# A transformer block on one core: the beginning reordered, tokens laid out by grid tiles, the first weights in pieces of 128 rows

## The chip, the core and the metric

The kernel runs on one core of a Trainium2 chip. A core has five engines with queues of their own: TensorE (PE; its weight loads are shown as PEld), VectorE (DVE), ScalarE (ACT), GpSimd (POOL) and SyncE (SP), which here only issues transfers. Sixteen DMA engines move data between HBM and the on-chip memory (SBUF). TensorE writes its products into PSUM, eight banks of 128 x 512 f32. The metric is the device time of one execution in microseconds (us).

## The reference

One layer of a block with modulation, for 1024 tokens (a grid of 16 rows by 64 columns) of width 1024 and 256 context tokens. What matters for the beginning:

```python
mod_x = (silu(c) @ w_mod + b_mod)            # six rows of 1024: sh1, sc1, gt1, sh2, sc2, gt2
mod_c = silu(c_ctx) @ w_mod + b_mod
h_x = rmsnorm(x, g_pre_mix) * (1 + sc1) + sh1
h_c = rmsnorm(ctx, g_pre_mix) * (1 + csc1) + csh1
u, q, k, v = split(h_x @ w_in)               # u: 512 columns, then three times 512
...
mix = concat(pool_mixer(u), neighbourhood_attention(q, k, v, k_ctx, v_ctx)) @ w_out
x = x + gt1 * rmsnorm(mix, g_post_mix)
x = x + gt2 * rmsnorm(relu(modulate(x) @ w_mlp_in)**2 @ w_mlp_out, g_post_mlp)
```

## The kernel before

All large products are made in three parts, since each operand is split into a high part (fp32r) and a low part: high x high, high x low, low x high (`three`, L197; in the beginning `some_sums`, L444). `high_part` (L144) is a copy on ScalarE, `low_part` (L150) a subtraction on VectorE.

The change lies in the beginning (L271 to L501), where the instructions of TensorE, ScalarE, VectorE, SP and GpSimd keep the order in which they are written (`in_order`, L104, entered at L284). It runs so:

- **Loads on SP** (L303 to L308): eight token tiles `x0` to `x7` of 128 tokens x 1024, 512 KB each; then, for each quarter q of the modulation, four pages of `w_mod` (`mod_load`, L297: 512 rows of K by 256 columns, for shift and scale) and the two K chunks 2q, 2q + 1 of `w_in`'s first 512 columns as one load (`raw_u`); then the context.
- **Normalisation**: a square with a running sum on ScalarE (`mean_square`, L130), then `rsqrt_of` (L133): an addition on VectorE and a power on GpSimd; then the tile is multiplied on VectorE (`normalised`, L333). `squares` of tile n + 1, with its inverse root, is written ahead of `normalised` of tile n (L368).
- **Transposes** on TensorE (`turned`, L343) of each 128 x 128 block, four tokens tiles side by side in a PSUM bank for each K chunk k and half h. `spare` (L339) puts transposes of the identity in between, whose results nobody reads.
- **Copies** out of PSUM (`by_bands`, L348) into `xT[k]`, 128 x 1024, on ScalarE or VectorE. The attention later works on tiles of 16 rows by 8 columns of the grid, so these copies also reorder the tokens from rows to such tiles. A token half `b` (512 columns of `xT`) needs both token halves of the input.
- **Modulation** of quarter q (256 of 1024 channels, K chunks 2q and 2q + 1 of the next product): `mod_sums` (L396) is 16 matmuls of `sT` (silu of c and c_ctx, 32 columns) against 256 columns; `mod_kept` copies the row; `shift_scale` (L415) turns it into columns by two small matmuls with `pck` (four PE instructions) and makes `a1` (scale) and `s1` (shift) by six small VectorE instructions.
- **`latent(b, k)`** (L431, through `modulated`, L202): ScalarE makes the high part, VectorE the f32 value and the low part; for b = 1 ScalarE also makes the f32 value and VectorE only the low part.
- **Products of u**: `some_sums(b, js, k)`, three matmuls of 128 x 512 for each of the output groups js: four for half 0, two for half 1, summed over k = 0 to 7 in the banks `pu`. The loop at L483 takes two values of k at a time, with the next quarter's modulation in between.

PSUM holds six banks that pass from tile to tile (`ps1`) and two for tiles named in `bank` (L273; `ps_t`, "lasting"). A tile that asks for a bank gets it when the one that had it has been read for the last time.

Later parts that the change touches: L548 to L550 rebuild `xT[0]` and `xT[1]` of half 0 by an addition (their f32 value was not kept in place), and the last stores (L1947) write rows back through the view `og` of the output.

Of the kernel before, what the change touches and what calls it, by code (L numbers as in the profile page):

```python
# [69 lines left out]

def _pick_table():
# [9 lines left out]
def hybrid_block(ctx, tc, x, ctx_in, w_mod, b_mod, gp1, gp2, w_in, pool_w, rpb, w_out, w1, w2, vectors,  # L81
# [37 lines left out]
    tiles = lambda a: a.rearrange("(r m c) d -> m r c d", r=QR, m=NM)  # L119
# [151 lines left out]
    with tc.tile_pool(name="ps1", bufs=6, space=PSUM) as ps1, tc.tile_pool(name="tmp1", bufs=3) as tmp:  # L271

        def bank(name):  # L273
            if name[:2] == "pm" or name in ("pxt1_0", "pxt0_2", "pxt1_7", "pct2", "pct3"):
                return lasting(name)
            return ps1.tile([P, 512], F32, tag="mm", name=name)
# [20 lines left out]
        def mod_load(q, kh, w):  # L297
            src = w_mod[:, w * D + q * 256 : w * D + (q + 1) * 256].rearrange("(h k p) f -> h p k f", p=P, h=2)
            t = page(f"wm{q}_{kh}_{w}")
            nc.sync.dma_start(t.rearrange("p (k f) -> p k f", k=4), src[kh])  # L300
            return t

        xn = [token_tile(f"x{n}", x[n * P : (n + 1) * P, :]) for n in range(NT)]  # L303
        wm, raw_u = [], []
        for q in range(4):
            wm.append([[mod_load(q, kh, w) for w in range(2)] for kh in range(2)])
            raw_u.append(load(f"wu{q}", pair(w_in, q, 0, 512)))
# [17 lines left out]
        inverse = {}  # L325

        def squares(name, t):
            jk = page(f"jk{name}")
            ms = sm(f"ms_{name}", 1, 4)
            mean_square(jk, t, ms)  # L330
            inverse[name] = rsqrt_of(f"t_{name}", ms)

        def normalised(name, t):  # L333
            nc.vector.tensor_scalar_mul(t, t, inverse[name])

        xT = [None] * KT

# [5 lines left out]
        def turned(pts, ns, ks):  # L343
            for k in ks:
                for n in ns:
                    nc.tensor.transpose(pts[k][:, (n % 4) * P : (n % 4 + 1) * P], xn[n][:, k * P : (k + 1) * P], ident)

        def by_bands(copy, h, ks):  # L348
            for k in ks:
                if xT[k] is None:  # L350
                    xT[k] = page(f"xT{k}")
                to = xT[k].rearrange("p (m r c) -> p m r c", m=NM, r=QR)[:, :, 8 * h : 8 * h + 8]
                copy(to, pts[h][k].rearrange("p (r m c) -> p m r c", m=NM, c=QC))


        on_act, on_dve = nc.scalar.copy, nc.vector.tensor_copy
        pts = [{}, {0: bank("pxt1_0")}]
        free = pts[1][0][:, 3 * P :]

        def turned_in(h, ns, ks):  # L360
            for k in ks:
                if k not in pts[h]:
                    pts[h][k] = bank(f"pxt{h}_{k}")
            turned(pts[h], ns, ks)

        spare(free, 30)
        squares("x0", xn[0])
        for n in range(NT):  # L368
            if n + 1 < NT:
                squares(f"x{n + 1}", xn[n + 1])  # L370
            if n == 5:
                by_bands(on_dve, 0, (0,))
            if n == 7:
                by_bands(on_dve, 0, (1,))
            normalised(f"x{n}", xn[n])
            if n < 4:
                turned_in(0, (n,), range(KT - 1))
        spare(free, 3)
        turned_in(1, (4,), (0,))
        spare(free, 10)  # L380
        turned_in(0, (0, 1, 2, 3), (7,))
        turned_in(1, (5,), (0,))
        spare(free, 3)
        by_bands(on_dve, 0, (2,))
        by_bands(on_act, 0, (3, 4, 5, 6, 7))
        turned_in(1, (4, 5), (4, 5))
        turned_in(1, (6,), (0, 4, 5))
        turned_in(1, (4, 5, 6), (1,))
        turned_in(1, (7,), (0, 1, 4, 5))
        turned_in(1, (4, 5, 6, 7), (6,))  # L390
# [5 lines left out]
        def mod_sums(q, pm, kh):  # L396
            for k in range(4 * kh, 4 * kh + 4):
                for w in range(2):
                    c = 2 * (k % 2) + w
                    o = (k % 4) * 256  # L400
                    nc.tensor.matmul(pm[32 * c : 32 * c + 32, :256], sT[:, k, :], wm[q][kh][w][:, o : o + 256],
                                     start=(k < 2), stop=(k >= KT - 2))

        def mod_kept(q, pm):
            mr = tmp.tile([P, 256], F32, tag="mrow", name=f"mrow{q}", bufs=2)
            nc.scalar.copy(mr, pm[:, :256])
            return mr
# [6 lines left out]

        def shift_scale(q, mr):  # L415
            pt = bank(f"pmt{q}")
            for j in range(2):
                nc.tensor.matmul(pt[:, 4 * j : 4 * j + 4], mr[:, j * P : (j + 1) * P], pck, start=True, stop=True)
            pv = pt[:, :8].rearrange("p (j w v) -> p w v j", w=2, v=2)
            hs = slice(2 * q, 2 * q + 2)  # L420
            for v in range(2):
                nc.vector.tensor_tensor(a1[v][:, hs], pv[:, 1, v], b_sc[:, hs], add)
                nc.vector.tensor_tensor(a1[v][:, hs], a1[v][:, hs], g1c[:, hs], mul)
                if q < 2:
                    nc.vector.tensor_tensor(s1[v][:, hs], pv[:, 0, v], b_sh[:, hs], add)
                else:
                    nc.vector.scalar_tensor_tensor(s1[v][:, hs], pv[:, 0, v], -1.0, b_sh[:, hs], mul, sub)
# [3 lines left out]
        def latent(b, k):  # L431
# [3 lines left out]
                      on_act=(b == 1), kept=src if b == 1 or k > 1 else None)  # L435
# [6 lines left out]
        pus = [[bank(f"pu{j}_{b}") for j in range(4 if b == 0 else 2)] for b in range(2)]  # L442

        def some_sums(b, js, k):  # L444
            h = hx[b][k]
# [17 lines left out]
        wu0h, wu0l = (whl.tile([P, 1024], F32R, tag="hl", name=f"wu0{n}") for n in "hl")  # L463
        by_bands(on_dve, 1, (0,))
        by_bands(on_act, 1, (1, 4, 5))
        by_bands(on_dve, 1, (6,))
        pm = bank("pm0")
        for kh in range(2):
            mod_sums(0, pm, kh)
        mr = mod_kept(0, pm)  # L470
        nc.scalar.copy(wu0h, raw_u[0])
        wgt.append((wu0h, wu0l))
        turned_in(1, (4, 5, 6, 7), (3,))
        shift_scale(0, mr)
        turned_in(1, (4, 5, 6, 7), (2, 7))
        nc.vector.tensor_tensor(wu0l, raw_u[0], wu0h.bitcast(F32), sub)
        latent(0, 0)
        latent(0, 1)
        by_bands(on_act, 1, (3, 2))
        by_bands(on_dve, 1, (7,))  # L480
        latent(1, 0)
        latent(1, 1)
        for q in range(4):  # L483
            some_sums(0, range(4), 2 * q)
            if q == 0:
                some_sums(0, (0, 1), 1)
            if q < 3:
                mr = mod_rows(q + 1)
                wgt.append(high_low(f"wu{q + 1}", raw_u[q + 1], 1.0 if q == 0 else -1.0))
            some_sums(0, range(2 if q == 0 else 0, 4), 2 * q + 1)  # L490
# [6 lines left out]
            if q == 2:  # L497
                for i, t in enumerate(cp):
                    squares(f"c{i}", t)
                for i, t in enumerate(cp):  # L500
                    normalised(f"c{i}", t)  # L501
# [46 lines left out]
        for k in range(2):  # L548
            hi, lo = hx[0][k][:, :512], hx[0][k][:, 512:]
# [1502 lines left out]
```

## Time and profile before

| | |
|---|---|
| median of 3 runs | 1027.59 us (1027.14 to 1028.0) |
| profiled execution | 1028.11 us, span 1026.3 us |
| PE busy | 1012.1 us, 5910 instructions |
| DVE busy | 746.8 us |
| ACT busy | 546.0 us |
| first transposes of tokens on PE | 8.07 us from the start |
| first product of u | 23.18 us |
| first product of k = 4 | 45.01 us |

In the profile's timeline each row has the start from the beginning of the span, the time that it took, the engine, the line, the operation, what is written from what, how many instructions are merged, and in brackets how long the engine stood idle before and what released it. In the windows each engine's busy time stands with its number of instructions, and the last three numbers are the granted clock of TensorE, the DMA engines' share and GB/s. In the groups, the numbers behind the bar are the busy time, the mean of one in ns, and the idle time before.

### The profile page before, as it was taken

Reading aid. Unit: us, or ns where it says so; the run is one execution under the profiler, and the core shown is the slowest. Engines: PE = TensorE matmul, PEld = TensorE weight load, DVE = VectorE, ACT = ScalarE, POOL = GpSimd, SP = SyncE. Lnnn points to the kernel's source line nnn. Section 1 sums busy time; section 2 is a strip of 40 time slices with the busy share of each in tenths; the row PEclk is TensorE's granted clock in tenths of the full one; section 3 lists DMA queues with packets and bytes.
Section 4 is the critical chain, followed back from the end, with each engine's and each line's share of the span. In section 5 each row is a group of like instructions: output and inputs, shape, how many; then the busy total and the mean of one; then the engine's idle time right before and its main releaser. Section 6 shows DMA issues by size and latency. Waiting matters only on the chain.

```text
span 1026.3 us, 16024 instructions
## 1 busy us (share of the span) xinstructions
PE 1012.1 (99%) x5910; PEld 839.0 (82%) x5910; DVE 746.8 (73%) x1156; ACT 546.0 (53%) x944; POOL 148.9 (15%) x230
## 2 busy tenths in 40 slices
PE   8999999999999999999999999999999999999997
PEld 6788888878898888888888888888888888888885
DVE  5588757977886688879998888755757666556576
ACT  7573254348896657776555554555543344334431
POOL 3011110156773321310000000000000000000001
PEclk9999999999999999999999999999999999999999
DMA  9999799623347966886776657537966766556556
GB/s 343 336 253 342 233 266 310 205 58 88 84 96 204 229 171 200 274 206 204 260 253 205 224 196 227 182 133 238 347 231 248 248 231 214 196 184 193 175 178 213
DMA packets 123134, 222.70 MB, mean 217 GB/s; under 512 B 9456, under 2 KB 55152, under 8 KB 123056
## 3 DMA queue, kind: packets, MB, share of 16 engines
q1 hardware_dynamic: 96560, 171.14, 50.7%
q0 software_dynamic: 9360, 19.58, 9.4%
q10 hardware_dynamic: 17136, 30.97, 8.1%
q8 instruction: 46, 0.75, 0.3%
q14 instruction: 32, 0.26, 0.1%
HBM read 168.16 MB, written 52.45 MB: 215 GB/s over the span
## 4 chain that ended last, share of the span: by engine, by line
PE 94%; DMA 2%; POOL 1%; ACT 1%; issue 1%; DVE 1%; SPq 0%; POOLq 0%; DVEq 0%; ACTq 0%
PE pu L449 4%; PE pa L1096 4%; PE phz L198 3%; PE phv L198 3%; PE pyx L198 3%; PE phx L198 3%; PE phx L200 3%; PE pyv L200 3%; PE pyx L200 3%; PE pyz L200 3%; PE pyv L199 3%; PE phz L199 3%; PE pyz L199 3%; PE phv L199 3%; PE phx L199 3%; PE phz L200 3%
## 5 line engine op out<-in xcount | busy, mean ns | idle before, releaser
L1042 ACT ACTIVATE sp<-sp,nm 128x640 f32<-128x640 f32 (+1 forms) x64 | 51.5, 805 | 9.6 <-DVE ri L1046 4.8
L1031 DVE CUSTOM_DVE_ANT_0 sp<-S,tab 128x640 f32<-128x640 f32 (+1 forms) x56 | 44.5, 794 | 14.1 <-PE pz L1062 10.3
L1638 ACT ACTIVATE c<-c 128x512 f32<-128x512 f32 x48 | 30.3, 631 | 45.9 <-DVE c L1758 25.7
L146 ACT CAST wpS<-S 128x512 fp32r<-128x512 f32 x64 | 38.8, 616 | 26.5 <-PE phv L200 9.9
L198 PE MATMUL phx<-thB,wpA 128*128 128x512 f32 x128 | 50.2, 392 | 0.0
L200 PE MATMUL phx<-thB,wpA 128*128 128x512 f32 x128 | 49.8, 389 | 0.0
L199 PE MATMUL phx<-tlB,wpA 128*128 128x512 f32 x128 | 49.8, 389 | 0.0
L152 DVE TENSOR_TENSOR wpS<-S,wpS 128x512 fp32r<-128x512 f32 x64 | 43.4, 685 | 7.6 <-ACT wpS L146 7.6
L140 POOL TENSOR_TENSOR ry<-vy,nhalf 128x1 f32<-128x1 f32 x8 | 5.9, 740 | 281.3 <-DVE vy L138 281.3
L1639 ACT ACTIVATE c<-c 128x512 f32<-128x512 f32 x48 | 30.3, 630 | 15.2 <-DVE sa L1721 12.1
L198 PEld LDWEIGHTS phx<-thB,wpA 128*128 128x128 f32 x128 | 24.0, 188 | 5.4 <-ACT s L1689 0.5
L200 PEld LDWEIGHTS phx<-thB,wpA 128*128 128x128 f32 x128 | 24.0, 188 | 5.0
L199 PEld LDWEIGHTS phx<-tlB,wpA 128*128 128x128 f32 x128 | 24.1, 188 | 4.8
L1081 DVE COPY pt<-T 128x512 f32<-128x512 f32 x32 | 21.9, 686 | 5.8 <-PE T L1062 5.8
L1096 PE MATMUL pa<-pt,v 128*64 128x128 f32 x352 | 25.9, 280 | 0.2
L198 PE MATMUL phz<-thB,wpS 128*128 128x512 f32 x64 | 25.0, 391 | 0.0
L198 PE MATMUL phv<-thT,wpA 128*128 128x512 f32 x64 | 25.0, 391 | 0.0
L199 PE MATMUL phz<-tlB,wpS 128*128 128x512 f32 x64 | 24.9, 390 | 0.0
L199 PE MATMUL phv<-tlT,wpA 128*128 128x512 f32 x64 | 24.9, 389 | 0.0
L200 PE MATMUL phz<-thT,wpS 128*128 128x512 f32 x64 | 24.9, 389 | 0.0
L200 PE MATMUL phz<-thB,wpS 128*128 128x512 f32 x64 | 24.9, 389 | 0.0
L200 PE MATMUL phv<-thT,wpA 128*128 128x512 f32 x64 | 24.9, 389 | 0.0
(1134 smaller groups left out, 3434.4 us busy)
## 6 DMA issues: line engine op xcount, KB each, us to landing
b<-in_w SPq DMA_DIRECT2D x64, 512.0 KB, 4.4
hrS<-hdS SPq DMA_DIRECT2D x32, 512.0 KB, 5.4
hrA<-hdA SPq DMA_DIRECT2D x24, 512.0 KB, 5.6
wm<-in_w_mod SPq DMA_DIRECT2D x16, 512.0 KB, 9.7
wa_0w<-in_w SPq DMA_DIRECT2D x16, 512.0 KB, 5.0
wa_1w<-in_w SPq DMA_DIRECT2D x16, 512.0 KB, 4.5
hdA<-c ACTq DMA_DIRECT2D x32, 256.0 KB, 2.9
hdS<-sa ACTq DMA_DIRECT2D x32, 256.0 KB, 3.2
```

What stands on the lines that cost most here:

```text
L146: nc.scalar.copy(hi, src)
L152: nc.vector.tensor_tensor(lo, src, hi.bitcast(F32), sub)
L198: nc.tensor.matmul(ps, ahi, bhi, start=first, stop=False, skip_group_check=more)
L199: nc.tensor.matmul(ps, ahi, blo, start=False, stop=False, skip_group_check=more)
L200: nc.tensor.matmul(ps, alo, bhi, start=False, stop=last, skip_group_check=more)
L449: nc.tensor.matmul(pus[b][j], wk(wgt, k, low, j * P, P), r, start=(k == 0 and n == 0), stop=(k == KT - 1 and n == 2))
L1031: nc.vector.tensor_tensor_reduce(out=to, in0=s, in1=bt, scale=1.0, scalar=BIG, op0=add, op1=ALU.min, accum_out=nm)
L1042: nc.scalar.activation(sp, sp, AF.Exp, bias=least[i, e], scale=-1.0, accum_out=sums[i][:, e : e + 1])
L1081: copy(turns[i].rearrange("p e i t -> p (e i) t")[:, :, h * HD : (h + 1) * HD], turned[i][h].rearrange("p (a t) -> p a t", a=8))
L1096: nc.tensor.matmul(pa[e * HD : (e + 1) * HD, cols], v[:, f : f + HD], turns[i][:, e, c] if c < 4 else fifths[i][:, :, (e + 1) * HD : (e + ...
L1638: nc.scalar.activation(r, src, AF.Relu)
L1639: nc.scalar.activation(r, r, AF.Square)
```

## The change

The host lays the tokens out by grid tiles (`_by_tiles`), so that a token tile of 128 rows is one tile of 16 by 8, and puts the result back (`_by_rows`). With that the first four token tiles are all that token half 0 needs. It also packs the modulation's first 2048 columns into pages (`_mod_pages`). For the quarters 0 and 1 such a page holds, for one chunk of 128 channels, 512 rows of K with shift and scale side by side.

In the kernel:

- Loads on SP: tiles 0 to 3; quarter 0 (two pages for the first chunk, half of the weight, two pages for the second, the other half); tiles 4 to 7; quarter 1 in the same pieces; quarters 2 and 3 as before, from the packed pages.
- The modulation of quarters 0 and 1 is made chunk by chunk: 16 matmuls with 128 columns, a copy of 128 columns, one small matmul (two PE instructions), and for each v two small VectorE instructions (`chunk_scale`).
- The weights of quarters 0 and 1 are split in halves of 512 (`half_weight`).
- The tokens of half 0 are transposed, copied, modulated and multiplied for k = 0 and 1 ahead of the transposes of half 1. Those use banks for two chunks and two tiles at a time (`second_turned`, `kept_two`), and one bank for chunk 6, then 7 (`last_chunk`).
- `rsqrt_of` is now called inside `normalised`, directly ahead of the multiplication.
- `latent` always keeps the f32 value in place; half 1 makes it on VectorE for k = 0 and 1. The additions at L548 to L550 are gone.

```diff
-    tiles = lambda a: a.rearrange("(r m c) d -> m r c d", r=QR, m=NM)
+    tiles = lambda a: a.rearrange("(m p) d -> m p d", p=P)
...
-            if name[:2] == "pm" or name in ("pxt1_0", "pxt0_2", "pxt1_7", "pct2", "pct3"):
+            if name[:2] == "pm" or name in ("pxt5", "pxb2", "pxb3", "pxb4", "pct2", "pct3"):
                 return lasting(name)
...
+        def mod_load(q, i, kh):
+            t = page(f"wm{q}_{i}_{kh}")
+            nc.sync.dma_start(t, mod_pages[4 * q + 2 * i + kh])
             return t
...
+        def first_loads(q):
+            raw_u[q] = wraw.tile([P, 1024], F32, tag="raw", name=f"wu{q}w")
+            for i in range(2):
+                for kh in range(2):
+                    wm[q][i][kh] = mod_load(q, i, kh)
+                nc.sync.dma_start(raw_u[q][:, i * 512 : (i + 1) * 512], w_in[(2 * q + i) * P : (2 * q + i + 1) * P, :512])
+
+        xn = token_tiles(0)
+        first_loads(0)
+        xn += token_tiles(1)
+        first_loads(1)
...
+        def normalised(n):
+            nc.vector.tensor_scalar_mul(xn[n], xn[n], rsqrt_of(f"t_x{n}", means[n]))
...
+        def chunk_scale(k, pt, v):
+            ks = slice(k, k + 1)
+            nc.vector.scalar_tensor_tensor(a1[v][:, ks], pt[:, 2 + v : 3 + v], b_sc[:, ks], g1c[:, ks], add, mul)
+            nc.vector.tensor_tensor(s1[v][:, ks], pt[:, v : v + 1], b_sh[:, ks], add)
...
-                      on_act=(b == 1), kept=src if b == 1 or k > 1 else None)
+                      on_act=(b == 1 and k > 1), kept=src)
...
+        spare(free, 30)
+        squared(0)
+        for n in range(4):
+            if n < 3:
+                squared(n + 1)
+            normalised(n)
+            if n < 3:
+                first_turned(n, range(KT - 1))
+                spare(free, 2)
         for kh in range(2):
+            mod_sums(0, whole[0], kh, 0)
+        mr = chunk_row(0)
+        first_turned(3, range(2))
+        picked(pt[0], mr, 0)
+        first_turned(3, range(2, KT - 1))
+        half_weight(0, 0, high_part)
+        put(on_dve, pxt[0], 0, 0)
+        chunk_scale(0, pt[0], 0)
+        half_weight(0, 0, low_part)
         latent(0, 0)
+        put(on_act, pxt[1], 1, 0)
+        put(on_act, pxt[3], 3, 0)
+        put(on_dve, pxt[2], 2, 0)
+        chunk_scale(0, pt[0], 1)
+        some_sums(0, (0, 1), 0)
+        chunk_sums(1, 0)
+        some_sums(0, (2, 3), 0)
+        chunk_sums(1, 1)
+        put(on_act, pxt[4], 4, 0)
+        put(on_dve, pxt[5], 5, 0)
+        mr = chunk_row(1)
+        half_weight(0, 1, high_part)
+        picked(pt[1], mr, 0)
+        chunk_scale(1, pt[1], 0)
+        half_weight(0, 1, low_part)
         latent(0, 1)
+        pxt[7] = bank("pxt7")
+        for n in range(4):
+            first_turned(n, (7,))
+        put(on_dve, pxt[6], 6, 0)
+        put(on_dve, pxt[7], 7, 0)
+        chunk_scale(1, pt[1], 1)
+        some_sums(0, range(4), 1)
...
+        for n in range(4, NT):
+            squared(n)
+        for n in (4, 5):
+            normalised(n)
+            second_turned(n, range(6))
+        chunk_sums(2, 0)
+        normalised(6)
+        kept_two(on_act, (0, 2, 3, 4), 4)
+        kept_two(on_dve, (1,), 4)
+        second_turned(6, range(4))
+        chunk_sums(2, 1)
+        normalised(7)
+        kept_two(on_dve, (5,), 4)
+        second_turned(7, range(4))
+        for n in (6, 7):
+            second_turned(n, (4, 5))
+        mr = chunk_row(2)
+        kept_two(on_act, (0,), 6)
+        kept_two(on_dve, (1,), 6)
+        picked(pt[2], mr, 0)
+        chunk_scale(2, pt[2], 0)
         latent(1, 0)
         latent(1, 1)
+        half_weight(1, 0, high_part)
+        half_weight(1, 0, low_part)
+        pus[1] += [bank(f"pu{j}_1") for j in range(2)]
+        kept_two(on_act, (2,), 6)
+        kept_two(on_dve, (3,), 6)
+        latent(0, 2)
+        chunk_scale(2, pt[2], 1)
+        some_sums(1, range(2), 0)
+        kept_two(on_act, (4,), 6)
+        kept_two(on_dve, (5,), 6)
+        last_chunk(6)
+        for kh in range(2):
+            chunk_sums(3, kh)
+        mr = chunk_row(3)
+        half_weight(1, 1, high_part)
+        half_weight(1, 1, low_part)
+        some_sums(1, range(2), 1)
+        picked(pt[3], mr, 0)
+        for v in range(2):
+            chunk_scale(3, pt[3], v)
+        latent(1, 2)
+        some_sums(0, range(4), 2)
+        last_chunk(7)
+        latent(0, 3)
+        latent(1, 3)
+        some_sums(1, range(2), 2)
+        mr = mod_rows(2)
+        wgt.append(high_low("wu2", raw_u[2], -1.0))
+        some_sums(0, range(4), 3)
+        shift_scale(2, mr)
+        some_sums(1, range(2), 3)
+        latents(2)
+        for q in (2, 3):
...
-        for k in range(2):
-            hi, lo = hx[0][k][:, :512], hx[0][k][:, 512:]
-            nc.vector.tensor_tensor(xT[k][:, :512], hi.bitcast(F32), lo.bitcast(F32), add)
...
-                        nc.sync.dma_start(og[m][:, :, cs], xt[:, cs])
+                        nc.sync.dma_start(og[m][:, cs], xt[:, cs])
```

More of the change, by code (lines that the diff above doesn't have):

```diff
@@ L378, in hybrid_block, with turned @@
[L378 to L390, printed above, removed]
+        def turned(to, n, k):
+            nc.tensor.transpose(to, xn[n][:, k * P : (k + 1) * P], ident)
@@ L441, in hybrid_block @@
         up = [None] * 4
-        pus = [[bank(f"pu{j}_{b}") for j in range(4 if b == 0 else 2)] for b in range(2)]
+        pus = [[], []]
         def some_sums(b, js, k):
+            if k == 0 and b == 0:
+                pus[0] += [bank(f"pu{j}_0") for j in js]
             h = hx[b][k]
@@ L476, in hybrid_block, with half_weight @@
[L476 to L480 removed]
+        wgt += [[whl.tile([P, 1024], F32R, tag="hl", name=f"wu{q}{n}") for n in "hl"] for q in range(2)]
+        def half_weight(q, i, part):
+            cs = slice(i * 512, (i + 1) * 512)
+            hi, lo = (t[:, cs] for t in wgt[q])
+            part(raw_u[q][:, cs], hi) if part is high_part else part(raw_u[q][:, cs], hi, lo)
```

164 lines of the change are left out of this document (82 added, 82 removed).

## The prediction

> **What bounds the kernel now.** I read the page first: engines, slices, chain.
>
> ```profile
> span 1026.3 us, 16024 instructions
> PE 1012.1 (99%) x5910; PEld 839.0 (82%) x5910; DVE 746.8 (73%) x1156; ACT 546.0 (53%) x944; POOL 148.9 (15%) x230
> PE   8999999999999999999999999999999999999997
> PE 94%; DMA 2%; POOL 1%; ACT 1%; issue 1%; DVE 1%; SPq 0%; POOLq 0%; DVEq 0%; ACTq 0%
> ```
>
> TensorE is full in every slice but the first and the last, and it is 94% of the chain. So a change of the beginning is worth what it moves TensorE's later work. Next came the windows of the beginning, cut at TensorE's first real transpose (8.06), at the first product of `u` (23.18), and at the first product of k = 4 (45.01).
>
> ```profile
> 0.00:8.06 8.06, 5.72 (x30) 5.49 (x30) 2.21 (x13) 4.43 (x7) 2.15 (x9) 1.00 0.79 283
> 8.06:23.18 15.12, 13.10 (x117) 10.13 (x117) 10.01 (x25) 12.22 (x24) 5.74 (x7) 1.00 1.07 373
> 23.18:45.01 21.83, 21.83 (x144) 16.39 (x145) 13.48 (x31) 13.33 (x20) 0.00 (x0) 1.00 1.08 362
> ```
>
> From 23.18 TensorE never rests. At 45.01 both kernels have done the same: 64 transposes, three quarters of the modulation and all products of k = 0 to 3; from there both issue the same lines. **The change is worth the shift of this point.** The timeline and the groups give the prices.
>
> ```profile
> 6.37 0.55 POOL L140 TENSOR_TENSOR rt_x<-vt_x,nhalf 128x1 f32<-128x1 f32 x1 [4.86 <-DVE vt_x L136]
> 7.26 0.75 DVE L334 TENSOR_SCALAR x<-x,rt_x 128x1024 f32<-128x1024 f32 x1
> 7.41 1.01 POOL L140 TENSOR_TENSOR rt_x<-vt_x,nhalf 128x1 f32<-128x1 f32 x1 [0.48 <-DVE vt_x L136]
> 7.21 1.06 ACT L131 ACTIVATE jkx<-x 128x1024 f32<-128x1024 f32 x1
> 8.49 1.06 ACT L131 ACTIVATE jkx<-x 128x1024 f32<-128x1024 f32 x1
> 15.65 0.68 DVE L353 COPY xT<-pxt 128x512 f32<-128x512 f32 x1
> 16.39 2.18 PE L346 MATMUL pxt<-ident,x 128*128 128x128 f32 x18 [0.69 <-DVE xT L353]
> 20.78 0.37 ACT L406 COPY mrow<-pm 128x256 f32<-128x256 f32 x1 [1.27 <-PE pm L401]
> 21.21 0.61 PE L418 MATMUL pmt<-cols,mrow 128*128 128x4 f32 x4
> 21.85 0.16 DVE L422 TENSOR_TENSOR a<-pmt,cols 128x2 f32<-128x2 f32 x1 [2.55 <-PE pmt L418]
> 22.31 1.52 ACT L208 ACTIVATE hx<-xT,s,a 128x512 fp32r<-128x512 f32 x2 [0.21 <-DVE s L425]
> 23.18 1.21 PE L449 MATMUL pu<-hx,wu0h 128*128 128x512 f32 x4 [0.43 <-ACT hx L208]
> 37.08 1.94 PE L401 MATMUL pm<-wm,sT 128*32 128x256 f32 x32
> 38.94 1.20 PE L449 MATMUL pu<-hx,wu1h 128*128 128x512 f32 x4
> 41.80 0.50 PE L418 MATMUL pmt<-cols,mrow 128*128 128x4 f32 x4
> 42.16 0.71 PE L449 MATMUL pu<-hx,wu1h 128*128 128x512 f32 x2
> 45.01 1.07 PE L449 MATMUL pu<-hx,wu2h 128*128 128x512 f32 x4
> 45.92 1.07 PE L449 MATMUL pu<-hx,wu2l 128*128 128x512 f32 x4
> ```
>
> ```profile
> L334 DVE TENSOR_SCALAR x<-x,rt_x 128x1024 f32<-128x1024 f32 x8 | 6.0, 751 | 0.0
> L210 DVE TENSOR_TENSOR hx<-xT,hx 128x512 fp32r<-128x512 f32 x8 | 5.4, 690 | 0.6 <-ACT hx L206 0.4
> L353 DVE COPY xT<-pxt 128x512 f32<-128x512 f32 x6 | 4.1, 685 | 0.3 <-PE pxt L346 0.3
> L209 DVE TENSOR_SCALAR xT<-xT,a,s 128x512 f32<-128x512 f32 x4 | 2.2, 545 | 1.1 <-ACT hx L208 1.1
> L136 DVE TENSOR_SCALAR vt_x<-ms_x 128x1 f32<-128x1 f32 x8 | 1.2, 154 | 3.2 <-ACT jkx L131 3.1
> L131 ACT ACTIVATION_READ_ACCUMULATOR jkx<-x 128x1 f32 x8 | 1.5, 186 | 0.0
> L353 ACT COPY xT<-pxt 128x512 f32<-128x512 f32 x10 | 5.1, 591 | 0.7 <-PE pxt L346 0.7
> L208 ACT ACTIVATE hx<-xT,s,a 128x512 fp32r<-128x512 f32 x6 | 4.6, 808 | 4.2 <-DVE s L427 2.4 <-DVE s L425 1.8
> L346 PE MATMUL pxt<-ident,x 128*128 128x128 f32 x64 | 9.1, 280 | 2.3 <-DVE x L334 1.7 <-DVE xT L353 0.7
> L406 ACT COPY mrow<-pm 128x256 f32<-128x256 f32 x3 | 1.1, 373 | 5.6 <-PE pm L401 5.6
> ```
>
> On TensorE a product follows the last by (45.92 - 45.01) / 4 = 0.23, a transpose by (2.18 - 0.28) / 17 = 0.11; a quarter's sums take 38.94 - 37.08 = 1.86 and four pick instructions 42.16 - 41.80 = 0.36. Real work in the 15.12 us before 23.18 is thus 64 x 0.11 + 1.86 + 0.36 = 9.3; the other 5.8 are fill transposes and waits, and bound the gain.
>
> **The change, step by step.** All times below are estimates from these rows, counted forward engine by engine, since each engine keeps the written order.
>
> *Start to first product.* The first four token tiles stay the first transfers, and the third and fourth squares start at 7.21 and 8.49 as before. New is that the inverse root is asked for directly before the normalisation, so VectorE waits for GpSimd: 0.15 + 0.09 + POOL + 0.06 + 0.75. POOL is unseen in that order; it took 0.55 with VectorE idle (6.37) and 1.01 with L334 running (7.41). VectorE is idle here: I take 0.55, 1.53 a tile counting the overlap of neighbours; the other end is 2.0. The Trainium skill, SBUF — State Buffer, "Who interferes with whom", says such VectorE operations fully block GpSimd. The two rows fit it; a flat 1.01 would add 4 x 0.46 = 1.8 in the second half.
>
> Transposes run at 7.8, 9.3 and 10.85, and the first chunk's sums at 11.8, by when its two pages are in: two more 512 KB transfers behind the fourth tile at one per 8.49 - 7.21 = 1.28. A chunk has all 16 products of a quarter at half the columns, an unseen shape: half of 1.86 if columns bind, 1.86 if the count does. I take 1.1, nearer the first; for four chunks the ends are 0 and +3.7 over two quarters. Row copy 13.15, pick 13.45 to 13.8, scale 14.05, ACT's high part 14.1 to 14.9: first product at **15.0**, not 23.18, a head start of 8.2.
>
> *To the second chunk.* The low part, which now works in place behind ACT's 14.94, ends at 14.94 + 0.06 + 0.64 + 0.69 = 16.35. The second chunk's sums need the long-lived PSUM bank of the first, free at 17.1, when VectorE has copied chunk 2 (0.68) and made the second scale; cut in two between six products each, they end at 19.7. The row copy and the pick follow, done at 20.7. TensorE waits 0.4 for the pick and 0.85 for the next high part, then issues twelve products to 24.6.
>
> *The loads.* SP issues one piece after the other, and the fifth token tile now stands behind four pages and two half weights: 4 x 1.28 + 2 x 0.64 = 6.4 later.
>
> ```profile
> 0.74 4.43 SPq L293 DMA_DIRECT2D x<-in_x  x8
> 5.21 6.42 SPq L300 DMA_DIRECT2D wm<-in_w_mod  x4
> ```
>
> From 9.8 (1.28 behind 8.49) that is 16.2, and 20.0 for the eighth. Their squares come on ACT behind the high part of k = 1, at 21.8, so this costs nothing; without that cover it would be up to 6.4. Two more issues at some 0.5 (4.43 / 8) lie inside the transfers' own pace.
>
> *VectorE's queue.* Here the gain goes. From 20.75 VectorE has in written order: scale 0.2, low half of a weight 0.7, modulated k = 1 1.4 (0.15 of it waiting for ACT), chunks 6 and 7 copied 1.25, scale 0.2; four serial normalisations 6.1; three half copies 1.2 (half of 0.68 and an overhead, an estimate between 0.34 and 0.68 each); 0.1 for the eighth tile's transposes; 0.8 for ACT's high part; modulated k = 0 and 1 of the second half, now here, 2.5; a low half 0.65; the copy of chunk 3 0.4. Sum 15.5, so **36.3**. ACT's squares take 1.06 + 0.19 each and stay ahead of it. Queued behind every GpSimd wait are these copies and modulated parts, and TensorE waits for them: 1.6 for the fifth tile (24.6 to 26.2), 0.9 for the sixth, 1.3 in pieces for the seventh and eighth, 0.5 for the high part. The second half's first product goes at 32.8; its neighbour wants a bank. Six short-lived banks hold four sums of the first half and two transposed pairs, and the second pair is free with the copy of chunk 3 at 36.3. That such bank waits are real shows at 16.39, where TensorE sat until the copy of 15.65 had ended. After five more products, at 37.5, chunk 6's transposes want one of the two long-lived banks: free at **37.8**, behind modulated (0, 2) 1.2 and a scale 0.25.
>
> *To k = 4.* From there TensorE is full: 8 transposes 0.9, a chunk 1.1, 42 products 9.5, a quarter 1.9, picks 0.6, and 0.6 for changes of kind and a last scale and high part that six products no longer cover (twelve did before). 37.8 + 14.6 = **52.4** against 45.01: **+7.4**.
>
> Counted the other way: 37.4 us from first product to k = 4 instead of 21.8, 15.6 more: 36 transposes 4.0, sums 1.5 (three chunks and a quarter for two quarters), picks and changes 0.8, waits 9.3. Less the 8.2.
>
> *At nothing:* the two additions that rebuilt xT (0.69 each by the L210 row) leave VectorE, and the context's normalisations now wait for GpSimd twice (0.7 each); both lie under TensorE's full stretch, and without cover they cancel. Strided copies become plain ones of the same count of elements: 0, ends -0.1 and 0 a copy. Token order on the host and in the last stores changes no bytes: 0, ends +-0.3.
>
> The profiled run took 1028.11, 1.8 over its span; 1028.11 + 7.4 = 1035.5. The median of the runs is 0.52 lower: **1035.0**. With POOL at its other end (+1.8), chunks at 0.93 or 1.86 (the one chunk behind 37.8 counts in full, those before it half: -0.4 to +1.9) and half copies at 0.34 with the second half's modulated parts better covered (-3): 1031 to 1039.
>
> **Rivals.** *Faster: the head start lasts.* Without any wait behind 11.8, TensorE has 43 x 0.11 + 4 x 1.1 + 1.9 + picks 1.2 + 72 x 0.227 + changes 1.5 = 30.0, so k = 4 at 41.8: -3.2, 1024.4. The place is VectorE's stretch from 20.75 to 37.8: break-even is 37.8 - 7.4 = 30.4, so it must take under 9.7 us instead of 17. For: VectorE idles some 3 us just before it, and the normalisations could slip there if the order did not bind. Against: normalisations, copies and modulated parts alone are 12.
>
> *No bank waits.* If chunk 3's bank or the long-lived one is free early, the low part at 34.2 holds instead: 3.2 less, +4.2, 1031.8. Against: the 16.39 row.
>
> *The clock falls.* The longest rest of TensorE that I count is 3.3, from 33 to 36.3.
>
> ```profile
> 1018.68 0.39 PE L200 MATMUL pyv<-t_7h,hhA_7l 128*128 128x512 f32 x1
> 1020.00:1022.00 2.00, 0.00 (x0) 0.00 (x0) 1.88 (x3) 0.00 (x0) 0.55 (x1) 1.00 0.00 0
> 1023.40:1026.30 2.90, 0.00 (x0) 0.00 (x0) 0.00 (x0) 0.00 (x0) 0.00 (x0) 0.50 0.38 134
> ```
>
> At the end the clock was whole until at least 1022 and half from 1023.4, over 3 us behind the last product. A fall would run some 4 us of work at half: +2, 1037.0. The Trainium skill, TensorE: Matmul & The Clock Gate, "Why this matters for your kernels", warns of gaps over about 3 us; by that the fall happens, by the row it just does not.
>
> *It does nothing:* transfers were not what the start waited for, and the new waits cancel: 1027.6.
>
> **Chances.** Forecast 0.55, no bank waits 0.12, clock 0.12, faster 0.18, nothing 0.03. The first three are slower by over 0.2% (2 us, what a measurement of this kernel can tell from none): 0.79; same 0.03; faster 0.18. The range 1024 to 1040 leaves out under half of the faster case and the far tails of the others, below 0.2 together. The likeliest case's own range stands above.
>
> **What will show it.** The first product near 15 and k = 4 near 52; TensorE's waits on VectorE's tokens near 25 and 27, on its copy near 36; POOL at 0.55 in all eight; the clock at 1.00. If k = 4 comes before 45, the queue on VectorE is the wrong step; if the first product comes after 18, the head start is. A time under 1027 makes the prediction wrong as a whole.

## The result, and the profile after

The changed kernel takes 1035.28 us (median of 6 runs, 1035.21 to 1035.89), the kernel before 1027.66 (6 runs, 1027.14 to 1029.1): a ratio of 1.0074, 95% interval 1.0061 to 1.0087. The profiled execution took 1035.89 us at a span of 1034.1, against 1028.11 and 1026.3: 7.8 more of each. The page of the changed kernel, engines, slices, granted clock and chain:

```profile
span 1034.1 us, 16150 instructions
PE 1015.3 (98%) x5964; PEld 840.4 (81%) x5964; DVE 748.6 (72%) x1166; ACT 544.7 (53%) x948; POOL 146.5 (14%) x230
PE   8799999999999999999999999999999999999997
PEclk9899999999999999999999999999999999999999
PE 95%; POOL 1%; ACT 1%; issue 1%; DVE 1%; DMA 0%; POOLq 0%; DVEq 0%; ACTq 0%
```

TensorE is still the chain. What is new is the 7 and the 8 in the second slice: rests, and a clock that was not whole (the kernel before has 9 in all forty slices of that row). The windows of the changed kernel, cut at its first product of `u`, at the second half's second product (36.36), at 42.84, which is 1.7 behind the moment when the clock was whole again, at k = 4, and at the last product of all:

```profile
14.98:36.36 21.38, 13.98 (x121) 9.38 (x121) 14.07 (x35) 12.26 (x26) 2.19 (x4) 0.95 1.03 408
36.36:42.84 6.48, 6.48 (x47) 4.98 (x48) 2.14 (x6) 1.93 (x4) 0.00 (x0) 0.63 1.03 398
42.84:54.33 11.49, 11.49 (x79) 8.50 (x77) 5.19 (x17) 5.60 (x10) 0.00 (x0) 1.00 0.25 81
54.33:1027.42 973.09, 970.84 (x5620) 807.02 (x5620) 718.90 (x1085) 516.67 (x895) 140.57 (x214) 1.00 0.66 211
```

The first product comes 8.2 us earlier, k = 4 comes 9.32 later (54.33 against 45.01). From there to the last product it takes 973.09 where it took 1018.68 - 45.01 = 973.67, and from the last product to the end 1034.1 - 1027.42 = 6.7 where it took 7.6. So 9.3 - 0.6 - 0.9 = 7.8. The timeline of the changed kernel shows where the head start went:

```profile
11.82 1.08 PE L399 MATMUL pm<-wm,sT 128*32 128x128 f32 x32
14.98 0.97 PE L453 MATMUL pu<-hx,wu0h 128*128 128x512 f32 x2 [0.71 <-ACT hx L231]
24.83 0.55 POOL L163 TENSOR_TENSOR rt_x<-vt_x,nhalf 128x1 f32<-128x1 f32 x1 [13.51 <-DVE vt_x L159]
25.42 0.75 DVE L383 TENSOR_SCALAR x<-x,rt_x 128x1024 f32<-128x1024 f32 x1 [0.73 <-POOL rt_x L163]
26.31 0.84 PE L368 MATMUL pxb<-ident,x 128*128 128x128 f32 x6 [1.32 <-DVE vt_x L159]
32.93 0.49 PE L453 MATMUL pu<-hx,wu0h 128*128 128x512 f32 x1 [0.53 <-ACT hx L231]
35.89 0.42 DVE L373 COPY xT<-pxb 128x256 f32<-128x256 f32 x1
36.36 0.80 PE L453 MATMUL pu<-hx,wu0h 128*128 128x512 f32 x1 [2.94 <-DVE xT L373]
38.66 1.06 PE L368 MATMUL pxb<-ident,x 128*128 128x128 f32 x4
54.33 1.19 PE L453 MATMUL pu<-hx,wu2h 128*128 128x512 f32 x4
```

The bracket is the idle time before an instruction. The row of 26.31 names `vt_x`, VectorE's addition before the next tile; the tile's normalisation is the instruction ahead of it on the same engine, and that ended last. The row of 36.36 is the largest rest: its releaser is the copy of 35.89, which reads a bank empty. A granted clock of 0.63 right behind it says that the work after the rest ran at half speed for a while. All of this is the profiled execution, the longest of the six; four of the others show a slightly higher mean clock (see the end), so their fall may have been shorter.

### The profile page after: what moved, and what is told of

It is laid out like the page before. It is cut to its first block, busy times and chain, and to the rows that moved or that the text cites. A ratio compares the mean times of both kernels' runs of the same rounds, so it can differ in the third digit from the quotient of the medians.

```text
span 1034.1 us, 16150 instructions
## 1 busy us (share of the span) xinstructions
PE 1015.3 (98%) x5964; PEld 840.4 (81%) x5964; DVE 748.6 (72%) x1166; ACT 544.7 (53%) x948; POOL 146.5 (14%) x230
## 4 chain that ended last, share of the span: by engine, by line
PE 95%; POOL 1%; ACT 1%; issue 1%; DVE 1%; DMA 0%; POOLq 0%; DVEq 0%; ACTq 0%
PE pu L453 4%; PE pa L1217 3%; PE phz L221 3%; PE phv L221 3%; PE phx L221 3%; PE pyx L221 3%; PE pyv L223 3%; PE phx L223 3%; PE pyx L223 3%; PE pyv L222 3%; PE pyz L223 3%; PE pyz L222 3%; PE phz L222 3%; PE phv L222 3%; PE phx L222 3%; PE phv L223 3%
## 5 line engine op out<-in xcount | busy, mean ns | idle before, releaser
L1152 DVE CUSTOM_DVE_ANT_0 sp<-S,tab 128x640 f32<-128x640 f32 (+1 forms) x56 | 44.5, 795 | 14.2 <-PE pz L1183 9.4
L1759 ACT ACTIVATE c<-c 128x512 f32<-128x512 f32 x48 | 30.3, 632 | 44.5 <-DVE c L1879 26.0
L222 PE MATMUL phz<-tlB,wpS 128*128 128x512 f32 x64 | 24.9, 390 | 0.0
L223 PE MATMUL phv<-thT,wpA 128*128 128x512 f32 x64 | 24.9, 389 | 0.0
L222 PE MATMUL phv<-tlT,wpA 128*128 128x512 f32 x64 | 24.9, 389 | 0.0
L223 PE MATMUL phz<-thB,wpS 128*128 128x512 f32 x64 | 24.9, 389 | 0.0
L221 PE MATMUL phy<-thT,wpS 128*128 128x512 f32 x64 | 24.9, 389 | 0.0
```

The costliest lines, as they stand in the source:

```text
L221: nc.tensor.matmul(ps, ahi, bhi, start=first, stop=False, skip_group_check=more)
L222: nc.tensor.matmul(ps, ahi, blo, start=False, stop=False, skip_group_check=more)
L223: nc.tensor.matmul(ps, alo, bhi, start=False, stop=last, skip_group_check=more)
L1152: nc.vector.tensor_tensor_reduce(out=to, in0=s, in1=bt, scale=1.0, scalar=BIG, op0=add, op1=ALU.min, accum_out=nm)
L1759: nc.scalar.activation(r, src, AF.Relu)
```

## The experiments

Each run has its own median against the kernel before, taken beside it. Times inside a kernel come from its one profiled execution, counted from the start of its span; there the first product of `u` stands between 14.95 (e8) and 15.37 (e2), apart from e4 and e5, so a few tenths between two runs say little. The first four change one thing of the changed kernel, the fifth changes only the stores of the kernel before, the rest follow from them.

**e1: the clock.** TensorE's rests between 24.9 and 36.4 are filled with transposes of the identity, into a long-lived bank that nobody reads.

```diff
-            if kh == 0:
+            if kh == 0 and k not in whole:
...
+        whole[2] = bank("pm1_0")
+        rest = whole[2][:, 128:256]
         for n in (4, 5):
             normalised(n)
+            spare(rest, 11 if n == 4 else 5)
             second_turned(n, range(6))
...
         chunk_sums(2, 1)
+        spare(rest, 2)
...
         chunk_scale(2, pt[2], 0)
+        spare(rest, 32)
         latent(1, 0)
```

> The changed kernel with 50 fill transposes of the identity more, in TensorE's rests between 24 and 36 us (11 ahead of the fifth tile's transposes, 5 ahead of the sixth's, 2 ahead of the eighth's, 32 ahead of the second half's first product). Nothing else moves. Theory (the clock of TensorE falls because the rests leave it too little work): granted clock 1.00 from 7 us to the end, products at 0.23 us apart behind 36.4, first product of k = 4 at about 52.2 instead of 54.33, time about 2 us below 1035.3. Rival (the slow products behind 36.4 come from the banks or from late weights, the clock row is only beside it): k = 4 stays at 54.3 and the time at 1035.3. Second rival (fill transposes delay the real ones): slower than 1035.3 by up to 1 us.

Windows of e1, cut at 14.98 as above (its own first product of `u` stands at 15.20), at the second half's second product and at k = 4:

```profile
14.98:36.46 21.48, 19.02 (x171) 14.66 (x171) 13.98 (x35) 12.48 (x27) 2.19 (x4) 1.00 1.03 407
36.46:52.64 16.18, 16.18 (x129) 12.00 (x127) 7.45 (x23) 7.53 (x13) 0.00 (x0) 1.00 0.59 223
```

The clock stays whole, the second product comes as late as before (36.46 against 36.36), and k = 4 comes at 52.64 instead of 54.33. The fall cost 1.7 us at k = 4 (from the second product on, 16.18 where it took 17.97); the rest of the shift has nothing to do with it. The time falls less, to 1034.79 us (4 runs; ratio 1.006, 1.0044 to 1.0077), where 2 were expected; its interval overlaps that of the changed kernel, so the 1.7 rests on the profiled execution. There 0.5 us went into a wait further down (below).

**e2: the bank.** All six copies of the second pair of tiles of half 1 (tiles 6 and 7), and the second scale of chunk 2, are written ahead of the modulated parts of half 1.

```diff
-        kept_two(on_act, (0,), 6)
-        kept_two(on_dve, (1,), 6)
+        kept_two(on_act, (0, 2, 4), 6)
+        kept_two(on_dve, (1, 3, 5), 6)
         picked(pt[2], mr, 0)
-        chunk_scale(2, pt[2], 0)
+        for v in range(2):
+            chunk_scale(2, pt[2], v)
         latent(1, 0)
         latent(1, 1)
...
-        kept_two(on_act, (2,), 6)
-        kept_two(on_dve, (3,), 6)
         latent(0, 2)
-        chunk_scale(2, pt[2], 1)
         some_sums(1, range(2), 0)
-        kept_two(on_act, (4,), 6)
-        kept_two(on_dve, (5,), 6)
```

> The changed kernel with the four copies of the second tile pair's chunks 2 to 5 and the second scale of chunk 2 written ahead of the modulated parts (1, 0) and (1, 1), so that the banks come free some 3 us earlier; VectorE's and ScalarE's work is the same. Theory (TensorE's rest to 36.36 is a wait for a bank): the two first products of the second half start one behind the other near 33.7, its low parts then hold to about 35; chunk 6's transposes at 35.5 instead of 38.66; k = 4 near 50 with the clock at 1.00, near 52.5 if it still falls; time 1031 to 1033.5. Rival (VectorE's modulated parts hold it, the bank is free anyway by then): second product still near 36, k = 4 at 54.3, time 1035.3.

TensorE in e2's timeline:

```profile
33.83 0.72 PE L453 MATMUL pu<-hx,wu0h 128*128 128x512 f32 x2 [1.05 <-ACT hx L231]
50.31 1.19 PE L453 MATMUL pu<-hx,wu2h 128*128 128x512 f32 x4
```

The two products now go together (x2), 0.9 later than the first alone and 2.5 earlier than the second. k = 4 is at 50.31, 4.0 earlier, and the clock is whole: with the shorter rest it does not fall in the profiled execution, which is 1.7 of the 4.0 by e1. The time is 1031.92 us (5 runs; ratio 1.0035, 1.0021 to 1.0048).

**e3: the inverse roots.** Each second-half tile's root is asked for one tile ahead of its use, as in the kernel before, so that VectorE does not stand still for GpSimd between normalisations.

```diff
+        def rooted(n):
+            inverse[n] = rsqrt_of(f"t_x{n}", means[n])
...
+        rooted(4)
         for n in (4, 5):
+            rooted(n + 1)
             normalised(n)
             second_turned(n, range(6))
         chunk_sums(2, 0)
+        rooted(7)
         normalised(6)
```

> The changed kernel with the inverse roots of tiles 4 to 7 asked for one tile ahead of the normalisation, as in the kernel before. Theory (three waits of 0.73 for GpSimd lie on the path): GpSimd's power takes about 1.0 beside L383 instead of 0.55, the normalisations follow at about 0.8 instead of 1.54, the copy that frees the bank ends about 2.1 earlier, k = 4 near 52.2, time 1033.2; more if the clock no longer falls. Rival (the waits are hidden behind ScalarE's copies and TensorE's transposes): time 1035.3, less 0.5 at most.

GpSimd, VectorE and TensorE in e3's timeline:

```profile
25.04 1.37 POOL L163 TENSOR_TENSOR rt_x<-vt_x,nhalf 128x1 f32<-128x1 f32 x2 [13.52 <-DVE vt_x L159]
30.82 0.42 DVE L373 COPY xT<-pxb 128x256 f32<-128x256 f32 x1 [1.10 <-ACT xT L373]
34.65 0.42 DVE L373 COPY xT<-pxb 128x256 f32<-128x256 f32 x1
53.47 1.19 PE L460 MATMUL pu<-hx,wu2h 128*128 128x512 f32 x4
```

The copy that frees the bank is at 34.65 instead of 35.89, so 1.24 is gained and not the 2.1 expected: part of it comes back as 1.10 of waiting at 30.82 for ScalarE's copy out of the same bank, which itself waits for the eighth tile's transposes (0.60 in the changed kernel). The clock fell here too (0.50 from 33.95 to 40.77), and k = 4 came only 0.86 earlier. 1034.7 us (4 runs; ratio 1.0059, 1.0044 to 1.0074).

**e4: the order of the loads.** All eight token tiles are loaded ahead of the first weights again; all else stays.

```diff
         xn = token_tiles(0)
+        xn += token_tiles(1)
         first_loads(0)
-        xn += token_tiles(1)
         first_loads(1)
```

> The changed kernel with all eight token tiles loaded first, as before; all else as changed. The first chunk's pages land behind the eighth tile, near 13.6 + 2.6 = 16.2. Theory (the order of the loads gives the head start, and everything behind it hangs on the first sums through a serial chain): first sums at 16.2 instead of 11.82, first product near 19.4 instead of 14.98, k = 4 later by 4.4 (58.7), time 1039.7, some 2 more if the clock falls in the longer rest. Rival (the head start is eaten by VectorE's queue anyway, so the load order is worth little): first product later, but k = 4 within 1 of 54.3 and time within 1 of 1035.3.

TensorE in e4's timeline:

```profile
15.40 1.08 PE L399 MATMUL pm<-wm,sT 128*32 128x128 f32 x16 [2.97 <-DMA wm<-in_mod_pages]
16.70 1.08 PE L399 MATMUL pm<-wm,sT 128*32 128x128 f32 x16 [0.23 <-DMA wm<-in_mod_pages]
20.01 1.27 PE L453 MATMUL pu<-hx,wu0h 128*128 128x512 f32 x2
61.69 1.19 PE L453 MATMUL pu<-hx,wu2h 128*128 128x512 f32 x4
```

and its windows around the first fall of the clock:

```profile
12.00:14.44 2.44, 0.42 (x4) 0.18 (x2) 0.64 (x1) 0.00 (x0) 0.00 (x0) 1.00 1.04 413
14.44:24.68 10.24, 8.97 (x65) 5.87 (x66) 4.11 (x10) 3.04 (x6) 0.00 (x0) 0.50 1.03 402
```

The first sums wait for their pages, and the first product comes 5.0 us later. k = 4 is at 61.69, 3.0 later than the 58.7 expected without a further fall of the clock: it fell a first time in the rest at 12 to 15 (0.50 from 14.44 to 24.68), and twice more. So the order of the loads is worth 3.6 us at the first sums and, with the halved clock behind them, 5.0 of the 8.2 at the first product; where the other 3.2 come from was not tried by itself. 1042.77 us (4 runs; ratio 1.0136, 1.0121 to 1.0151).

**e5: the stores alone.** The kernel before, with rows kept as they were at the beginning and only the result laid out by tiles, so that each last store writes one block of 128 rows.

```diff
-    xg, og = tiles(x), tiles(out)
+    xg, og = tiles(x), out.rearrange("(m p) d -> m p d", p=P)
...
-                        nc.sync.dma_start(og[m][:, :, cs], xt[:, cs])
+                        nc.sync.dma_start(og[m][:, cs], xt[:, cs])
```

> The kernel before with one edit: the last stores write token tiles of 128 rows in one piece (the host puts the rows back), as the changed kernel does; the input stays in rows. Theory (the 0.93 us by which the changed kernel's end is shorter, 6.69 instead of 7.62 from the last product to the end of the span, comes from the stores' form): the last issues on SP take 0.33 instead of 0.54, the end is 6.7, time 0.9 below the kernel before. Rival (the end is shorter for another reason, as which queue or address the store meets): end 7.6, time unchanged.

The end in the timelines, the kernel before, e5 and the changed kernel:

```profile
1021.49 1.20 SPq L1947 DMA_DIRECT2D out<-xo  x2
```

```profile
1019.19 0.39 PE L205 MATMUL pyv<-t_7h,hhA_7l 128*128 128x512 f32 x1
1022.00 0.99 SPq L1952 DMA_DIRECT2D out<-xo  x2
```

```profile
1027.42 0.39 PE L223 MATMUL pyv<-t_7h,hhA_7l 128*128 128x512 f32 x1
1030.23 0.99 SPq L2068 DMA_DIRECT2D out<-xo  x2
```

In all three the last two stores are issued 2.81 us behind the last product. In the kernel before they take SP 1.20 and the end is 1026.3 - 1021.49 = 4.8 later; with the tiles 0.99, and 4.0 and 3.9. So 0.8 to 0.9 us of the end comes from the form of the stores. 1027.0 us against 1027.99 (11 and 27 runs; ratio 0.9991, 0.9982 to 1.0). It is the only version that came out below the kernel before, and its interval reaches to no change.

**e6: bank and roots together,** the edits of e2 and e3.

> The changed kernel with the early copies and the early roots together (the edits of the two runs before). Theory (VectorE's queue and the bank are one serial chain): the savings add, 4.0 from the copies and 1.3 to 2.1 from the roots, k = 4 at 48.2 to 49.0, clock 1.00, time 1030 to 1030.7. Rival (behind the early copies ScalarE or TensorE's own sums and transposes bind): k = 4 at 50.3 and time 1031.9 as with the copies alone.

k = 4 in e6's timeline, and its windows, the last line adding up the three before:

```profile
48.59 1.20 PE L460 MATMUL pu<-hx,wu2h 128*128 128x512 f32 x4
```

```profile
14.98:24.95 9.97, 8.62 (x62) 5.62 (x62) 6.26 (x17) 6.00 (x12) 0.02 (x1) 1.00 1.03 411
24.95:34.00 9.05, 6.48 (x66) 4.70 (x66) 6.93 (x19) 6.36 (x16) 3.20 (x4) 1.00 1.03 404
34.00:48.59 14.59, 14.59 (x122) 10.90 (x120) 8.04 (x21) 7.53 (x13) 0.00 (x0) 1.00 0.82 311
sum 33.61, PE 29.69 PEld 21.22 DVE 21.23 ACT 19.89 POOL 3.22; mean PE 9.90 PEld 7.07 DVE 7.08 ACT 6.63 POOL 1.07
```

5.7 us of the 9.3 are back; 1029.99 us (10 runs; ratio 1.0018, 1.0009 to 1.0027). Behind e2's edit the roots are worth 1.7 at k = 4 (50.31 to 48.59), or 1.4 counted from each run's own first product; alone they gave 0.9, or 1.1 counted so.

The sum line says more: in the 33.61 us TensorE is busy for 29.69 and rests for 3.9. Had it no rest at all, k = 4 would stand at 14.98 + 29.69 = 44.7, against 45.01 before. That is an estimate, and a late one: ahead of each rest the last product counts to its modelled end (0.49 for the single one at 32.93 in the changed kernel), where in a full stretch the next one follows after 0.23. Counted the other way, from the kernel before, which needs 45.01 - 23.18 = 21.83 from its first product to k = 4 without a rest: there now lie 36 transposes more (4.0 at 0.11 each), three chunks and a quarter of sums instead of two quarters (1.5 at 1.1 a chunk and 1.86 a quarter), and their picks (0.2), some 27.5 in all, which would put k = 4 at 42.5. So in this layout an earlier first product has between 0.3 and 2.5 us to give, because the work behind it has grown; no order that was tried came near it.

**e7: another order,** written to take those rests away: the fifth tile is squared and normalised, and its transposes are made, ahead of the products of k = 1; k = 2 of half 0 goes ahead of half 1; all copies of a pair of tiles stand together, and roots ahead as in e3. The edit is long; these are parts of it.

```diff
         put(on_act, pxt[4], 4, 0)
         put(on_dve, pxt[5], 5, 0)
+        squared(4)
+        squared(5)
...
+        rooted(4)
+        normalised(4)
+        put(on_dve, pxt[7], 7, 0)
         mr = chunk_row(1)
...
         latent(0, 1)
+        second_turned(4, range(6))
         some_sums(0, range(4), 1)
...
+        latent(0, 2)
...
+        some_sums(0, range(4), 2)
         latent(1, 0)
         latent(1, 1)
```

> The changed kernel in another written order, with the same work: the fifth tile squared, normalised and transposed in the rests before the second chunk's pick, the roots one tile ahead, all copies of a tile pair together, chunk 2 of the first half multiplied ahead of the second half's chunk 0. Theory (the waits of the written order, not the loads or the pieces, take back the head start): TensorE rests under 3 us between 15 and k = 4, k = 4 near 44.5, time 1026, 1.5 below the kernel before. Rival (the pieces and serial waits cost it in any order): k = 4 not under 48, time above 1029.5. In between: the new order has waits of its own that I have not counted.

ScalarE and TensorE in e7's timeline:

```profile
18.52 1.06 ACT L154 ACTIVATE jkx<-x 128x1024 f32<-128x1024 f32 x1 [2.07 <-DMA x<-in_x]
20.85 0.25 ACT L410 COPY mrow<-pm 128x128 f32<-128x128 f32 x1
23.09 1.19 PE L460 MATMUL pu<-hx,wu0h 128*128 128x512 f32 x4 [0.44 <-ACT hx L231]
31.93 1.20 PE L460 MATMUL pu<-hx,wu1l 128*128 128x512 f32 x4 [0.72 <-DVE wu1l L175]
48.10 1.19 PE L460 MATMUL pu<-hx,wu2h 128*128 128x512 f32 x4 [0.47 <-ACT hx L231]
```

It missed its 44.5 and came out near its rival, with k = 4 at 48.10. The rows show waits that were not counted: the fifth tile lands only at 18.5, the two squares then stand ahead of the second chunk's row copy on ScalarE, and a low weight is late at 31.93. 1029.13 us (11 runs; ratio 1.0014, 1.0005 to 1.0023), the best of the orders tried and still 1.1 above the kernel before.

**e8: e7 with the squares behind.** The squares and the normalisation of the fifth tile move behind `latent(0, 1)`, its transposes behind the products of k = 1.

```diff
-        squared(4)
-        squared(5)
...
-        rooted(4)
-        normalised(4)
-        put(on_dve, pxt[7], 7, 0)
         mr = chunk_row(1)
...
         latent(0, 1)
+        squared(4)
+        squared(5)
+        rooted(4)
+        normalised(4)
+        put(on_dve, pxt[7], 7, 0)
         chunk_scale(1, pt[1], 1)
-        second_turned(4, range(6))
         some_sums(0, range(4), 1)
+        second_turned(4, range(6))
```

> The order of the run before (e7), but the squares and the normalisation of the fifth token tile stand behind the second chunk's row copy, weight and modulated part, and its transposes behind the products of k = 1. Theory: in e7 the token tile landed at 18.5, and its two squares on ACT pushed the row copy from 20.1 to 20.85 and the first product of k = 1 from 22.07 to 23.09. With them behind it, the row copy is at 20.1, the first product of k = 1 at 22.1, TensorE goes on without a rest to the fifth tile's transposes at about 24.9, and k = 4 comes 1.0 earlier than e7: 47.1, the time about 1028.1. Rival: the later waits of e7 (the low weight, the normalisations of the sixth to eighth tile) end at the same moment whatever the start: k = 4 at 48.0 to 48.3, the time 1029.1. In neither case is it ahead of 45.0, because TensorE's own work from the first product takes 29.7 us by the e6 rows (15.06 + 29.7 = 44.8) and some rests stay.

TensorE and VectorE in e8's timeline:

```profile
21.95 1.21 PE L460 MATMUL pu<-hx,wu0h 128*128 128x512 f32 x4 [1.27 <-ACT hx L231]
26.34 0.76 DVE L390 TENSOR_SCALAR x<-x,rt_x 128x1024 f32<-128x1024 f32 x1 [0.67 <-POOL rt_x L163]
49.12 1.20 PE L460 MATMUL pu<-hx,wu2h 128*128 128x512 f32 x4 [0.46 <-ACT hx L231]
```

Both theories missed. The first product of k = 1 did come 1.1 us earlier, and yet k = 4 came 1.0 later: 1030.67 us (8 runs; ratio 1.0027, 1.0016 to 1.0038). The sixth tile's normalisation, at 26.34 here, was at 25.33 in e7, and everything behind it shifted by the same 1.0. Between these two orders it is VectorE's passage through the second half's tiles that sets k = 4, and not when TensorE begins k = 1.

## Why the prediction was right, and where it was not

**The head start** was right: first sums 11.82 for 11.8, first product 14.98 for 15.0, GpSimd 0.55 in all eight roots, a chunk of sums 1.08 for 1.1. The Trainium skill, SBUF — State Buffer, "Who interferes with whom", has a VectorE operation that takes both of its ports block GpSimd fully while it runs; VectorE stood idle beside each of these roots, so they agree. e4 shows that 5.0 of the 8.2 come from the order of the loads.

**VectorE's queue and the bank** were right: 24.6 to 26.2 was put as the fifth tile's wait (26.31 measured), 32.8 for the second half's first product (32.93), 36.3 for the end of the copy that frees a bank (35.89 + 0.42), 37.8 for chunk 6's transposes (38.66, the products ahead of them at half the clock). e2 shows that this bank was what TensorE waited for, by taking the copy ahead. The rival without bank waits is out. e8 shows that in another order the same queue still sets k = 4. One term of that step was too early and cost nothing: the fifth tile was put at 16.2, and in e7, with the same loads, ScalarE waited for it until 18.52; in the changed kernel its square comes at 21.83, so 3.3 of cover were left.

**The clock** was a rival with a chance of 0.12 and +2; a fall of 1.7 happened beside the forecast, not in place of it. The step that failed is the reading of the kernel's end, that a fall takes a rest of over 3 us. The windows of the changed kernel around the fall, 3.41 us each:

```profile
24.06:27.47 3.41, 1.78 (x11) 1.07 (x9) 1.95 (x7) 2.03 (x4) 1.10 (x2) 1.00 1.03 405
27.47:30.89 3.42, 2.68 (x42) 1.82 (x42) 1.96 (x6) 1.20 (x4) 1.10 (x2) 1.00 1.03 410
30.89:34.30 3.41, 1.71 (x11) 1.31 (x11) 2.58 (x8) 2.87 (x7) 0.00 (x0) 1.00 1.04 399
34.30:37.71 3.41, 1.35 (x3) 1.17 (x4) 3.34 (x9) 1.03 (x3) 0.00 (x0) 0.50 1.02 406
37.71:41.12 3.41, 3.41 (x35) 2.58 (x38) 0.30 (x1) 0.59 (x1) 0.00 (x0) 0.50 1.04 403
```

The clock (third number from the right) was halved at 34.30, with the long rest hardly a microsecond old: the window that ended there had been busy for only 1.71 of 3.41. It stayed halved behind the next, also thin window (1.35), and was whole again behind a full one. The end of the kernel before, counted in the same steps, fits this as well: TensorE was busy for 2.55 of the step to 1019.94 and for none of the next, and the clock fell at 1023.35, where that one ended. Both falls come at the end of a thin step, with a rest of 0.9 us behind the last product here and of 4.3 there. Filling the rests (e1) kept it whole, and so did shortening them (e2), in the profiled executions. By e1's 52.64 the clock has 1.7 of the 9.3 at k = 4, and the queue and the bank the other 7.6, for which the sum had 7.4.

**The end** was put at 0, ends +-0.3: mis-sized. The stores in one block of rows are worth 0.8 to 0.9 us, shown in e5 by themselves.

**The stretch from k = 4 on** was taken as unchanged; it is 0.6 shorter. In the kernel before and in e5, TensorE waits at one place in the middle of the kernel for VectorE (the rows of the kernel before and of e5):

```profile
351.57 0.47 PE L198 MATMUL poz<-to_0h,S 128*128 128x512 f32 x1 [0.32 <-DVE ns L1454]
352.09 0.47 PE L203 MATMUL poz<-to_0h,S 128*128 128x512 f32 x1 [0.67 <-DVE ns L1459]
```

The changed kernel, e2, e3, e4, e6, e7 and e8 have no such wait; e1 has it. Product by product, the changed kernel lies 9.3 behind the kernel before at k = 4, 9.4 to 9.5 from there up to that place, and 8.7 from that place to the last product, so the gain lies there. It was not tried what sets this wait, so its cause stays open.

**The sum.** 1035.0 was forecast and 1035.28 measured, for the profiled execution 1035.5 and 1035.89, but not wholly for the reasons given: about 1.7 of clock that was not in the forecast stands against the 1.5 that the end and the stretch from k = 4 gave back. The faster rival was priced too early as well: it put k = 4 at 41.8 without any rest, where the two counts at e6 give 42.5 to 44.7. About 1.0 of that lies between the first sums and the first product, 11.82 to 14.98: a chain of copy, pick and modulated part takes 3.16 there, with some 2.2 of counted work on TensorE. The inverse roots, 2.1 by the serial waits that e3 was to remove, gave 0.9 to 1.2, and with e2's edit 1.4 to 1.7.

## What to carry to other kernels

An earlier first product is worth only what the engine behind it can keep up with: add up the bound engine's own work from there to a point that both versions share, and see first how much earlier an arrival is possible at all (here 42.5 to 44.7 against 45.01), then whether the engine that feeds it, in its written order, gets there. Write a copy that empties a bank ahead of work that nobody waits for yet; here that move was worth 3.4 us, with the clock's fall that did not come in the profiled execution. And look at how busy the matrix engine is in each few microseconds, not only at its longest rest: thin stretches can cost the clock.

## What the runs showed of the hardware

- The granted clock moved in steps of 3.41 us: halved for 6.83 us (34.30 to 41.12) in the changed kernel, for 6.82 in e3, for 10.24, 3.41 and 6.83 in e4. The ten traces, cut into such steps from the clock's first rise on, have 15 falls, each at the end of a step in which TensorE was busy for 1.74 us or less (1.71 in the changed kernel, 1.12 in e3, 1.20, 1.52 and 1.74 in e4, 0.8 or less at the kernels' ends). Steps without a fall had 1.78 or more, but for the steps up to 1021.28 in e5 (1.72) and up to 1023.67 in e6 (1.77). So the border, if it is one of busy time, lies near half a step; busy times are modelled, and a few hundredths between them say nothing. The way back took more: the clock rose again only behind a step that was full, and stayed halved behind 2.24 (e3), 2.23 and 3.32 (e4). The Trainium skill, TensorE: Matmul & The Clock Gate, "What's actually happening", describes a free-running window of 3413 ns; the lengths agree. The Trainium skill's warning of gaps over about 3 us, on the same page in "Why this matters for your kernels", does not tell this fall: the rest in which it came was a microsecond old. The six executions of the changed kernel show mean clocks of 0.995 to 0.997, and those at 0.995 (1035.77 and 1035.89) are the longest. One of e4's steps, with the clock fallen behind it at 41.74:

```profile
38.33:41.74 3.41, 1.74 (x15) 1.31 (x11) 2.28 (x6) 3.14 (x7) 0.00 (x0) 1.00 1.04 402
```

- The same bytes stored as one block of 128 rows, instead of rows of the grid in pieces, occupied SP for 0.99 us where two stores had taken 1.20, and were done 0.8 us sooner behind their issue.
- Two requests for an inverse root made together took GpSimd 1.37 us (e3), beside a normalisation of 0.75 on VectorE; alone one takes 0.55.
